# Delta-net opening: modulation groups pinned behind the products, small vectors turned sooner, first low parts of weights on VectorE

## Chip, cores and metric

One core of one Trainium2 chip runs the whole program. The metric is the device time of one execution in microseconds (us); lower is better. Engines: PE is TensorE, DVE is VectorE, ACT is ScalarE, POOL is GpSimd, SP is SyncE, which issues most of the transfers.

## What is computed

Two transformer blocks of two layers each, on 256 tokens of width 1024, all in float32. The part that matters here is the first layer of the first block:

```python
cond = jax.nn.silu(c)
mod = cond @ w_ada[layer] + b_ada[layer]                 # (1, 6144)
sh1, sc1, g1, sh2, sc2, g2 = jnp.split(mod[:, None, :], 6, axis=-1)
h = rms_norm(x, norm_mix[layer]) * (1.0 + sc1) + sh1
proj = h @ w_in                                          # gated delta net: (256,1024) @ (1024,4112)
qkv, z, a, b = jnp.split(proj, ...)
qkv = silu(causal_depthwise_conv(qkv, conv_w))           # 4 taps
...
```

The second block has its own modulation, `silu(c) @ w_ada[i] + b_ada[i]` and the same for `c_ctx`, from inputs that are there from the start, and ends each layer with a mixture of 16 experts.

## The kernel before

The program is written in Bass with the Tile framework. Its scheduler sets the order of the instructions of each engine from a simulated timeline. An instruction given to `keep_in_program_order` stays behind those of its engine that were written before it; instructions written under `issue_after(i)` come after instruction `i`.

**Exact products.** A product of float32 numbers is made of three products of parts: each weight is split by `split_w` (L380 to L392) into a high part `whi`, a cast on ACT (L387), and a low part `wlo`, a subtraction (L391) on VectorE, or on GpSimd where the counter `pool_next` is above zero (`gdn` sets it to 4 at L552) and for a share of all splits. The activations are split in the same way into `hi` and `lo`. The three matmuls of the delta net are L601 (hi by whi), L602 (hi by wlo) and L603 (lo by whi).

**The opening.** `rows_to_cols` and `runs_to_cols` (L168 to L194) load small vectors as rows and turn them into columns on PE (L178, L191) with a copy on VectorE (L180, L193): `va` and `vf` are the gains of the norms, `cw` the taps of the convolution; `al` comes of a matmul by ones in `gdn_consts` (L523). Meanwhile `ada_unit` makes the first third of the first layer's modulation: eight weight tiles of 128 x 2048 (1 MB each) are loaded by `load_w` (L135) into the raw buffers, and each goes through four matmuls of 32 rows (L218), called a group here. Then VectorE adds the bias (L244, `brow`), PE turns the result (L248), VectorE copies it (L250, `modc`) and forms the scale A (L364). `turned_early` has by then put the normed, turned x into PSUM; `modulated` makes `hi` on ACT (L371) and `lo` on VectorE in pairs (L372, L373).

**The delta net's projections** (`gdn`, L586 to L606) run over column blocks of 512 columns. A block has two raw tiles of 1 MB; each tile is split in two halves, and a half (two chunks of 128 rows by four of 128 columns) serves 24 matmuls, so that a block holds 96. After each block come the convolution of its columns (`conv`, ACT L559, VectorE L561), squares and, for later blocks, turns (L575, L580). Six such blocks are followed by `dense` for the rest.

**Background work.** `self.bg` is a list of generators; `fill` takes the next step of the first. While the delta net runs, the background is `ada2(0, 0)`, the second block's first modulation unit (`two` is true: eight groups of L218 that gather in one PSUM bank), and then further units on ACT and GpSimd.

**Buffers and queues.** All raw tiles come from one pool of five buffers in this stage (two, and `more_raw(3)`), shared by the delta net's weights and the modulation's. SP issues their loads one after another: a load whose buffer isn't free holds up the loads behind it. A delta-net tile's buffer comes free when its second low part is made, a modulation tile's when its group has run on PE.

Of the kernel before, what the change touches and what calls it, by code (L numbers as in the profile page):

```python
# [20 lines left out]
P = 128  # L21
# [11 lines left out]
class Kern:  # L33
# [134 lines left out]
    def rows_to_cols(self, name, srcs, eng=None):  # L168

        nc = self.nc  # L170
        n = sum(s.shape[0] for s in srcs)
# [5 lines left out]
        tp = self.tp()  # L177
        nc.tensor.transpose(tp[:, :n], r[:n, :P], self.ident[:n, :n])  # L178
        t = self.c.tile([P, n], F32, name=name)
        nc.vector.tensor_copy(t, tp[:, :n])  # L180
        return t

    def runs_to_cols(self, name, src, eng):

        nc = self.nc
        n = src.shape[0]
        r = self.t512()
        eng.dma_start(r[:n, :], src)
        tp = self.tp()
        for j in range(4):  # L190
            nc.tensor.transpose(tp[:, n * j:n * j + n], r[:n, j::4], self.ident[:n, :n])  # L191
        t = self.c.tile([P, 4 * n], F32, name=name)
        nc.vector.tensor_copy(t.rearrange("p (r j) -> p j r", j=4), tp[:, :4 * n].rearrange("p (j r) -> p j r", j=4))  # L193
        return t  # L194
# [11 lines left out]
    def ada_unit(self, w, b, unit, lhs, modc, two, dve=None, then=None, pool=False):  # L206
# [4 lines left out]
        if dve is None:  # L211
            bank = self.bank("ada")
            for k in range(KT):
# [3 lines left out]
                for j in range(4):  # L217
                    nc.tensor.matmul(bank[32 * j:32 * j + 32, :], lhs[:, k, :],  # L218
                                     r[:, 0, 512 * j:512 * j + 512], start=(k == 0), stop=(k == 7))
# [289 lines left out]
    def gdn_consts(self, bp):  # L509

        nc, I = self.nc, self.I
        am = self.t512()
        nc.gpsimd.dma_start(am[:, :2 * P], I["k_add"])
        mbf = bp.tile([P, 2 * P], BF16, name="mbf")
        nc.vector.tensor_copy(mbf, am[:, 0:2 * P])
        ibf = bp.tile([P, P], BF16, name="ibf")
        nc.vector.tensor_copy(ibf, self.ident)
# [4 lines left out]
        tp = self.tp()  # L522
        nc.tensor.matmul(tp[:, 0:16], self.ones[0:1, :], row, start=True, stop=True)  # L523
        nc.vector.tensor_copy(al[:, 0:16], tp[:, 0:16])
        cw = self.rows_to_cols("cw", [I["gdn_conv"][0].rearrange("a (r p) -> (a r) p", p=P), I["gdn_out_norm"]], nc.gpsimd)
        return mbf, ibf, al, cw

    def gdn(self, x, hi, lo, g1, consts, later):
# [3 lines left out]
        with ExitStack() as es:  # L532
# [19 lines left out]
            self.pool_next = 4  # L552
# [69 lines left out]
            self.banks("b", [2, 3], [], [7], [5])  # L622
            self.even_consts()
# [1368 lines left out]
    def prep(self):  # L1992
# [10 lines left out]
        self.va = self.rows_to_cols("va", [rv2(I[n]) for n in ("norm_mix", "norm_ffn", "norm_mix_2")], nc.gpsimd)  # L2003
        self.vf = self.runs_to_cols("vf", I["norm_ffn_2"].rearrange("l (h n) -> (l h) n", h=2), nc.gpsimd)
# [53 lines left out]
    def block1_layers(self, hp, modc, gb, ada, gmix, gffn):  # L2058
        I, x = self.I, self.x
        for l in range(2):  # L2060
            hi = hp.tile([P, KT, NTOK], F32R, name=f"hi{l}", tag="hi")
            lo = hp.tile([P, KT, NTOK], F32R, name=f"lo{l}", tag="lo")
            if l == 0:
                self.bg = [ada(0, 0, False)]
                consts = self.gdn_consts(self.accp)
                with self.more_raw(6), self.tc.tile_pool(reuse_waits="tile", name="xn", bufs=1, side="right") as xp:
                    early = self.turned_early(x, xp)
                    self.fill(5)
# [89 lines left out]
```

## Time and profile before

| | before |
|---|---|
| median of 3 runs | 2452.18 us (2449.21 to 2452.27) |
| profiled execution, its own time | 2443.09 us |
| span of the profiled execution | 2441.3 us |
| mean granted clock of PE | 0.941 |
| PE busy | 2123.6 us (87%) |
| VectorE busy | 1100.0 us (45%) |
| ScalarE busy | 773.9 us (32%) |
| GpSimd busy | 316.8 us (13%) |
| moved by DMA | 677.57 MB, mean 278 GB/s |

The time of an execution is a little above its span, which runs from the first to the last instruction. The profiled execution was 9 us below the median of the runs. A busy time is a union over an engine's instructions; the granted clock is a share of full speed (2.4 GHz), so 0.50 is 1.2 GHz. Line numbers in the profile are those of the kernel before; in the changed kernel the same lines have moved down by 3 to 13: L218 is L226 there, L244 is L254, L248 is L258, L372 and L373 are L382 and L383, L391 is L401, L387 is L397, L601 to L603 are L609 to L611.

### The profile page before, as it was taken

To read this page: it belongs to the slowest core of one execution; us is meant where nothing else is said; L and a number is where in the kernel's file an instruction comes from. 1 tells how busy PE (TensorE), PEld (TensorE's weight loads), DVE (VectorE), ACT (ScalarE), POOL (GpSimd) and SP (SyncE) were. 2 spreads that over 40 slices of the span, in tenths; PEclk is the share of its full clock that TensorE was granted. 3 is DMA by queue.
4 is the path that set the end of the run, shared out by engine and by line. 5 is a ranking of instruction groups with operands and counts; after the bars stand their busy time and mean duration, and the time that the engine had idled before them with its cause. 6 is when DMAs were issued, how large, how long until landed. Compare 5 with 4: busy or idle time off the path is not lost. (4 is left out here: it accounts for less than half of the span.)

```text
span 2441.3 us, 30277 instructions
## 1 busy us (share of the span) xinstructions
PE 2123.6 (87%) x12053; PEld 1278.1 (52%) x12053; DVE 1100.0 (45%) x2051; ACT 773.9 (32%) x1470; POOL 316.8 (13%) x334
## 2 busy tenths in 40 slices
PE   6987998998999979998988998888888987777777
PEld 3864676786677657885575222222265652222222
DVE  3777357866555575547764121212157731101111
ACT  3564344443555544435443100000047530000000
POOL 3344211112000040003411000000021010000000
PEclk8988998999999979999998999999989989989999
DMA  9657766976332356537746999999921469999998
GB/s 351 247 174 240 238 226 218 362 256 215 126 109 85 126 189 203 167 119 264 296 169 267 425 426 427 425 426 426 415 84 63 162 274 426 426 426 425 427 425 349
DMA packets 152445, 677.57 MB, mean 278 GB/s; under 512 B 15937, under 2 KB 38315, under 8 KB 113648
## 3 DMA queue, kind: packets, MB, share of 16 engines
q1 hardware_dynamic: 143072, 637.98, 67.3%
q0 software_dynamic: 6784, 36.48, 4.3%
q8 instruction: 95, 1.56, 0.3%
q10 hardware_dynamic: 2448, 1.18, 0.2%
q14 instruction: 46, 0.38, 0.0%
HBM read 667.07 MB, written 8.52 MB: 277 GB/s over the span
## 5 line engine op out<-in xcount | busy, mean ns | idle before, releaser
L391 DVE TENSOR_TENSOR wlo<-rawt,whi 128x1024 fp32r<-128x1024 f32 (+2 forms) x257 | 308.7, 1207 | 228.0 <-ACT whi L387 225.6
L387 ACT CAST whi<-rawt 128x1024 fp32r<-128x1024 f32 (+3 forms) x284 | 280.5, 995 | 313.7 <-PE mmt L398 118.9
L1872 PE MATMUL anyt<-rawb,xs 128*32 128x512 f32 x672 | 164.4, 650 | 52.0 <-DMA rawb<-in_w_exp_gate 26.7
L1858 PE MATMUL anyt<-rawb,xs 128*32 128x512 f32 x1472 | 175.2, 614 | 26.6 <-DMA rawb<-in_w_exp_up 17.3
L1832 DVE TENSOR_TENSOR y<-anyt,g 32x512 f32<-32x512 f32 (+1 forms) x120 | 66.4, 553 | 214.7 <-PE anyt L1825 206.9
L1825 PE MATMUL anyt<-rawb,hT 128*32 128x256 f32 (+1 forms) x1056 | 132.9, 491 | 21.2 <-DMA rawb<-in_w_exp_down 11.0
L398 PE MATMUL anyt<-whi,lo 128*128 128x512 f32 (+1 forms) x384 | 144.8, 379 | 1.8 <-DVE lo L333 1.8
L397 PE MATMUL anyt<-wlo,hi 128*128 128x512 f32 (+1 forms) x384 | 145.4, 380 | 1.1 <-DVE wlo L391 1.1
L1877 DVE TENSOR_TENSOR h<-anyt,h 64x512 f32<-64x512 f32 x16 | 11.1, 693 | 281.8 <-ACT h L1876 281.8
L396 PE MATMUL anyt<-whi,hi 128*128 128x512 f32 (+1 forms) x384 | 134.4, 381 | 0.4 <-ACT t L1723 0.4
L1876 ACT ACTIVATE h<-anyt 64x512 f32<-64x512 f32 x16 | 9.4, 589 | 392.4 <-PE anyt L1872 392.4
L1862 ACT ACTIVATE h<-anyt 128x512 f32<-128x512 f32 x16 | 9.6, 597 | 378.1 <-PE anyt L1858 378.1
L1872 PEld LDWEIGHTS anyt<-rawb,xs 128*32 128x32 f32 x672 | 39.3, 118 | 171.0 <-issue 100.7
L1858 PEld LDWEIGHTS anyt<-rawb,xs 128*32 128x32 f32 x1472 | 48.8, 112 | 147.1 <-issue 113.4
L1863 DVE TENSOR_TENSOR h<-anyt,h 128x512 f32<-128x512 f32 x16 | 11.1, 692 | 207.8 <-PE anyt L1858 207.8
L1825 PEld LDWEIGHTS anyt<-rawb,hT 128*32 128x32 f32 (+1 forms) x1056 | 49.5, 128 | 94.3 <-issue 65.0
L218 PE MATMUL adat<-rawt,lhs 128*32 128x512 f32 x448 | 73.6, 665 | 29.0 <-DMA rawt<-in_w_ada 24.9
L391 POOL TENSOR_TENSOR wlo<-rawt,whi 128x1024 fp32r<-128x1024 f32 (+1 forms) x27 | 67.6, 2511 | 237.7 <-ACT whi L387 196.2
L1872 PE MATMUL anyt<-rawt,xs 128*32 128x512 f32 x352 | 78.7, 596 | 10.9 <-DMA rawt<-in_w_exp_gate 7.3
L397 PEld LDWEIGHTS anyt<-wlo,hi 128*128 128x128 f32 x384 | 72.5, 189 | 20.5 <-issue 3.2
L398 PEld LDWEIGHTS anyt<-whi,lo 128*128 128x128 f32 x384 | 72.4, 188 | 16.2 <-DVE lo L333 2.2
L396 PEld LDWEIGHTS anyt<-whi,hi 128*128 128x128 f32 x384 | 71.6, 189 | 16.6 <-issue 0.8
(634 smaller groups left out, 4381.2 us busy)
## 6 DMA issues: line engine op xcount, KB each, us to landing
rawt<-in_w_ada SPq DMA_DIRECT2D x96, 1024.0 KB, 7.0
rawb<-in_w_exp_up SPq DMA_DIRECT2D x41, 2048.0 KB, 27.0
rawb<-in_w_exp_down SPq DMA_DIRECT2D x41, 2048.0 KB, 27.0
rawb<-in_w_exp_gate SPq DMA_DIRECT2D x39, 2048.0 KB, 25.6
rawt<-in_w_exp_gate SPq DMA_DIRECT2D x41, 1024.0 KB, 26.5
rawt<-in_w_ffn_in SPq DMA_DIRECT2D x40, 1024.0 KB, 7.7
rawt<-in_w_exp_up SPq DMA_DIRECT2D x38, 1024.0 KB, 27.0
rawt<-in_w_exp_down SPq DMA_DIRECT2D x31, 1024.0 KB, 27.0
```

The lines of the kernel that those rows point to most:

```text
L218: nc.tensor.matmul(bank[32 * j:32 * j + 32, :], lhs[:, k, :], r[:, 0, 512 * j:512 * j + 512], start=(k == 0), stop=(k == 7))
L387: nc.scalar.copy(hi, w)
L391: e.tensor_tensor(out=lo, in0=w, in1=hi.bitcast(F32), op=OP.subtract)
L396: nc.tensor.matmul(ps, xh, wh, start=start, stop=False)
L397: nc.tensor.matmul(ps, xh, wl, start=False, stop=False)
L398: nc.tensor.matmul(ps, xl, wh, start=False, stop=stop)
L1825: nc.tensor.matmul(yb[o:o + M, c:c + n], hT[:, k, :], w[:, i * n:i * n + n], start=(k == 0), stop=(k == KT - 1), **({} if S == 2 else dict ...
L1832: nc.vector.tensor_tensor(out=ys[s][p0:p0 + CAP, 256 * q:256 * (q + n)], in0=yb[o:o + CAP, c:c + 256 * n], in1=g2[o:o + CAP, 256 * q:256 * ...
L1858: nc.tensor.matmul(b[CAP * i:CAP * i + CAP, :], lhs(k0 + j, i % 2), r[:, j, 512 * hf:512 * hf + 512], start=(k0 + j == 0), stop=(k0 + j == ...
L1863: nc.vector.tensor_tensor(out=h, in0=banks[1], in1=h, op=OP.mult)
L1872: nc.tensor.matmul(b[o:o + 32, :], lhs(k0 + j), r[:, j, 512 * hf:512 * hf + 512], start=(k0 + j == 0), stop=(k0 + j == KT - 1), tile_posit ...
L1877: nc.vector.tensor_tensor(out=h[0:64, :], in0=b[64:P, :], in1=h[64:P, :], op=OP.mult)
```

## The change

1. `rows_to_cols(later=True)`, `runs_to_cols` and `gdn_consts` no longer turn their vectors where they load them; they give back a `turn` function. `block1_layers` calls these for `va`, `vf`, `al` and `cw` right after `turned_early`, with the PE instructions kept in program order, and lets most of the first modulation unit come after the last of them.
2. In `ada_unit`, where `two` is true, the four matmuls of the first group (k = 0) are kept in program order. Since the eight groups gather in one bank, the others follow the first.
3. `k_add`'s load and the casts `mbf` and `ibf` move from `gdn_consts` to the end of the projections.
4. `pool_next = 4` is gone: the first four low parts are made on VectorE.

```diff
--- before.py
+++ after.py
@@ -165,7 +165,7 @@
         self.tc.keep_in_program_order(self.nc.scalar.preload_act_table_set("natural_log_exp_and_others"))
 
 
-    def rows_to_cols(self, name, srcs, eng=None):
+    def rows_to_cols(self, name, srcs, eng=None, later=False):
 
         nc = self.nc
         n = sum(s.shape[0] for s in srcs)
@@ -174,24 +174,32 @@
         for s in srcs:
             (eng or nc.sync).dma_start(r[o:o + s.shape[0], :P], s)
             o += s.shape[0]
-        tp = self.tp()
-        nc.tensor.transpose(tp[:, :n], r[:n, :P], self.ident[:n, :n])
         t = self.c.tile([P, n], F32, name=name)
-        nc.vector.tensor_copy(t, tp[:, :n])
-        return t
+
+        def turn():
+            tp = self.tp()
+            i = nc.tensor.transpose(tp[:, :n], r[:n, :P], self.ident[:n, :n])
+            if later:
+                self.tc.keep_in_program_order(i)
+            nc.vector.tensor_copy(t, tp[:, :n])
+            return i if later else t
+        return (t, turn) if later else turn()
 
     def runs_to_cols(self, name, src, eng):
+
 
         nc = self.nc
         n = src.shape[0]
         r = self.t512()
         eng.dma_start(r[:n, :], src)
-        tp = self.tp()
-        for j in range(4):
-            nc.tensor.transpose(tp[:, n * j:n * j + n], r[:n, j::4], self.ident[:n, :n])
         t = self.c.tile([P, 4 * n], F32, name=name)
-        nc.vector.tensor_copy(t.rearrange("p (r j) -> p j r", j=4), tp[:, :4 * n].rearrange("p (j r) -> p j r", j=4))
-        return t
+
+        def turn():
+            tp = self.tp()
+            for j in range(4):
+                self.tc.keep_in_program_order(nc.tensor.transpose(tp[:, n * j:n * j + n], r[:n, j::4], self.ident[:n, :n]))
+            nc.vector.tensor_copy(t.rearrange("p (r j) -> p j r", j=4), tp[:, :4 * n].rearrange("p (j r) -> p j r", j=4))
+        return t, turn
 
 
     def ada_bias(self, b, c0, two):
@@ -215,8 +223,10 @@
                     yield
                 r = self.load_w(w[k * P:k * P + P, c0:c0 + 2048], 1, 2048)
                 for j in range(4):
-                    nc.tensor.matmul(bank[32 * j:32 * j + 32, :], lhs[:, k, :],
-                                     r[:, 0, 512 * j:512 * j + 512], start=(k == 0), stop=(k == 7))
+                    i = nc.tensor.matmul(bank[32 * j:32 * j + 32, :], lhs[:, k, :],
+                                         r[:, 0, 512 * j:512 * j + 512], start=(k == 0), stop=(k == 7))
+                    if two and k == 0:
+                        self.tc.keep_in_program_order(i)
         else:
             bank = self.bank("ada")
             for h in range(2):
@@ -509,20 +519,19 @@
     def gdn_consts(self, bp):
 
         nc, I = self.nc, self.I
-        am = self.t512()
-        nc.gpsimd.dma_start(am[:, :2 * P], I["k_add"])
         mbf = bp.tile([P, 2 * P], BF16, name="mbf")
-        nc.vector.tensor_copy(mbf, am[:, 0:2 * P])
         ibf = bp.tile([P, P], BF16, name="ibf")
-        nc.vector.tensor_copy(ibf, self.ident)
         al = bp.tile([P, 24], F32, name="al")
         row = bp.tile([1, 16], F32, name="alrow")
         nc.gpsimd.dma_start(row[:, 0:8], I["gdn_a_log"])
         nc.gpsimd.dma_start(row[:, 8:16], I["gdn_dt_bias"])
-        tp = self.tp()
-        nc.tensor.matmul(tp[:, 0:16], self.ones[0:1, :], row, start=True, stop=True)
-        nc.vector.tensor_copy(al[:, 0:16], tp[:, 0:16])
-        cw = self.rows_to_cols("cw", [I["gdn_conv"][0].rearrange("a (r p) -> (a r) p", p=P), I["gdn_out_norm"]], nc.gpsimd)
+
+        def turn():
+            tp = self.tp()
+            self.tc.keep_in_program_order(nc.tensor.matmul(tp[:, 0:16], self.ones[0:1, :], row, start=True, stop=True))
+            nc.vector.tensor_copy(al[:, 0:16], tp[:, 0:16])
+        cw, tw = self.rows_to_cols("cw", [I["gdn_conv"][0].rearrange("a (r p) -> (a r) p", p=P), I["gdn_out_norm"]], nc.gpsimd, True)
+        self.turns += [turn, tw]
         return mbf, ibf, al, cw
 
     def gdn(self, x, hi, lo, g1, consts, later):
@@ -549,7 +558,6 @@
             esd.enter_context(self.more_raw(3, "right", "gdn"))
 
             self.accv = dp
-            self.pool_next = 4
             a0 = self.bg[0]
             self.bg.insert(0, self.prep2_step(hi[:, 0, 0:1].bitcast(F32)))
 
@@ -620,6 +628,10 @@
             self.use_exp_ln()
             self.banks("a", [0, 1], [4], [6], [5])
             self.banks("b", [2, 3], [], [7], [5])
+            am = self.t512()
+            nc.gpsimd.dma_start(am[:, :2 * P], I["k_add"])
+            nc.vector.tensor_copy(mbf, am[:, 0:2 * P])
+            nc.vector.tensor_copy(ibf, self.ident)
             self.even_consts()
             cp = es.enter_context(tc.tile_pool(reuse_waits="tile", name="ctxp", bufs=1))
 
@@ -2000,8 +2012,9 @@
         x = self.c.tile([P, 2, D], F32, name="x")
         self.x = x
         nc.scalar.dma_start(x, I["x"][0].rearrange("(t p) d -> p t d", p=P))
-        self.va = self.rows_to_cols("va", [rv2(I[n]) for n in ("norm_mix", "norm_ffn", "norm_mix_2")], nc.gpsimd)
-        self.vf = self.runs_to_cols("vf", I["norm_ffn_2"].rearrange("l (h n) -> (l h) n", h=2), nc.gpsimd)
+        self.va, ta = self.rows_to_cols("va", [rv2(I[n]) for n in ("norm_mix", "norm_ffn", "norm_mix_2")], nc.gpsimd, True)
+        self.vf, tf = self.runs_to_cols("vf", I["norm_ffn_2"].rearrange("l (h n) -> (l h) n", h=2), nc.gpsimd)
+        self.turns = [ta, tf]
         lhs = self.c.tile([P, 8, 2, 16], F32, name="lhs2")
         nc.vector.tensor_copy(lhs, sc[:, 8:24].rearrange("p (s k) -> p k s", s=2).unsqueeze(3).to_broadcast([P, 8, 2, 16]))
         self.lhs2 = lhs.rearrange("p k s r -> p k (s r)")
@@ -2065,7 +2078,11 @@
                 consts = self.gdn_consts(self.accp)
                 with self.more_raw(6), self.tc.tile_pool(reuse_waits="tile", name="xn", bufs=1, side="right") as xp:
                     early = self.turned_early(x, xp)
-                    self.fill(5)
+                    for turn in self.turns:
+                        last = turn()
+                    self.fill()
+                    with self.tc.issue_after(last.ins):
+                        self.fill(4)
             m = modc[l][:, 0, :]
             if l:
                 self.norm_T(x, gmix(l), m[:, 8:16], m[:, 0:8], hi, lo, (0, 1))
```

What moves is seen in the order of the instructions on three engines (the scheduler sets it anew).

PE around the first products: `adat` with `lhs1` is the first layer's modulation, `adat` with `lhs2` the second block's, `tpt` a turn, `mmt` with `whi` or `wlo` a product. Before:

```order
L218 MATMUL adat_234<-rawt_271,lhs1_115 32x512 x4
L178 MATMUL tpt_95<-cst_68,t512_91 128x48
L523 MATMUL tpt_138<-alrow_135,cst_68 128x16
L218 MATMUL adat_234<-rawt_277,lhs1_115 32x512 x4
L191 MATMUL tpt_101<-cst_68,t512_99 128x4 x4
L248 MATMUL tpt_284<-cst_68,brow_231 128x128 x4
L178 MATMUL tpt_144<-cst_68,t512_141 128x97
L218 MATMUL adat_684<-rawt_685,lhs2_108 32x512 x4
L601 MATMUL mmt_355<-hi0_126,whi_359 128x256
```

After the change, the same place, and behind the line of dots what stands behind the 288th product:

```order
L181 MATMUL tpt_224<-cst_68,t512_125 128x97
L226 MATMUL adat_230<-rawt_243,lhs1_106 32x512 x4
...
L226 MATMUL adat_230<-rawt_273,lhs1_106 32x512 x4
L258 MATMUL tpt_280<-cst_68,brow_227 128x128 x4
L609 MATMUL mmt_351<-hi0_117,whi_355 128x256
...
L226 MATMUL adat_680<-rawt_681,lhs2_99 32x512 x4
L226 MATMUL adat_680<-rawt_687,lhs2_99 32x512 x4
L226 MATMUL adat_680<-rawt_693,lhs2_99 32x512 x4
L226 MATMUL adat_680<-rawt_699,lhs2_99 32x512 x4
L588 MATMUL tpt_833<-cst_68,kT_338 128x128 x2
```

The four turns stand ahead of the second modulation group; the first group of the second block's unit has gone from ahead of the first product to behind 288 products, and the other seven with it: four stand there together, one 24 products later, three within the 24 after that. Before, one stood ahead of the products, one within the first block, two behind 192 products and four behind 288.

SP's loads from the second block's third weight tile on (`in_w_ada_2` is the second block's modulation, `in_gdn_w_in` the delta net's weights; in brackets the DMA queues and engines whose count the issue waits for). Before:

```order
L135 DMA rawt_711<-in_gdn_w_in 128x4x512 [waits DMAHW6_49,DMAHW1_49,PE_49]
L135 DMA rawt_697<-in_w_ada_2 128x2048 [waits DMAHW7_49,Pool_49]
L135 DMA rawt_883<-in_w_ada_2 128x2048 [waits DMAHW2_49,DMAHW0_49,PE_49]
L135 DMA rawt_703<-in_w_ada_2 128x2048 [waits DVE_49]
L135 DMA rawt_769<-in_gdn_w_in 128x4x512 [waits DVE_49]
L135 DMA rawt_901<-in_w_ada_2 128x2048 [waits DMAHW6_49,DMAHW3_49,DVE_49]
L135 DMA rawt_889<-in_w_ada_2 128x2048 [waits DMAHW7_49,DMAHW4_49,PE_49]
L135 DMA rawt_895<-in_w_ada_2 128x2048 [waits DMAHW5_49,DMAHW1_49,PE_49]
L135 DMA rawt_917<-in_gdn_w_in 128x4x512 [waits DMAHW2_49,DVE_49]
L135 DMA rawt_1110<-in_gdn_w_in 128x4x512 [waits DMAHW6_49,DVE_49]
L135 DMA rawt_975<-in_gdn_w_in 128x4x512 [waits DMAHW0_49,PE_49]
```

After:

```order
L135 DMA rawt_693<-in_w_ada_2 128x2048 [waits DMAHW6_49,DVE_49]
L135 DMA rawt_699<-in_w_ada_2 128x2048 [waits DMAHW7_49,DVE_49]
L135 DMA rawt_707<-in_gdn_w_in 128x4x512 [waits DMAHW0_49,DVE_49]
L135 DMA rawt_765<-in_gdn_w_in 128x4x512 [waits DMAHW1_49,DMAHW0_49,DVE_49]
L135 DMA rawt_897<-in_w_ada_2 128x2048 [waits DMAHW2_49,DMAHW1_49,DVE_49]
L135 DMA rawt_913<-in_gdn_w_in 128x4x512 [waits DMAHW3_49,PE_49]
L135 DMA rawt_879<-in_w_ada_2 128x2048 [waits DMAHW4_49,PE_49]
L135 DMA rawt_885<-in_w_ada_2 128x2048 [waits DMAHW6_49,DMAHW5_49,PE_49]
L135 DMA rawt_891<-in_w_ada_2 128x2048 [waits DMAHW7_49,PE_49]
L135 DMA rawt_1106<-in_gdn_w_in 128x4x512 [waits DMAHW3_49,DVE_49]
L135 DMA rawt_971<-in_gdn_w_in 128x4x512 [waits DMAHW4_49,PE_49]
```

The third block's two tiles (711 and 769 before, 707 and 765 now) have moved behind two modulation loads. 707 now waits for the last low part of the second block (`wlo_609`), 765 for the last low part of 707 itself (`wlo_738`), so for the buffer that 707 had. The fourth block's first tile (917, now 913) waited for VectorE and now waits for the first pinned group (`rawt_681`); its second tile (975, now 971) waits for the fifth group, `rawt_879` (before, for its counterpart 883, which ran earlier).

VectorE at the opening (`brow` is the bias add, `wlo` a low part). Before:

```order
L180 COPY va_97<-tpt_95 128x48
L524 COPY al_134<-tpt_138 128x16
L193 COPY vf_106<-tpt_101 128x4x4
L515 CAST mbf_130<-t512_128 128x256
L244 TENSOR_TENSOR brow_231<-adat_234,brow_231 128x512
L250 COPY modc0_117<-tpt_284 128x4x4
L364 SCALAR_TENSOR_TENSOR smt_297<-modc0_117,va_97 128x8
L372 TENSOR_SCALAR t512_299<-hi0_126,modc0_117 128x256
```

After:

```order
L201 COPY vf_98<-tpt_215 128x4x4
L401 TENSOR_TENSOR wlo_356<-rawt_353,whi_355 128x1024
L532 COPY al_121<-tpt_221 128x16
L401 TENSOR_TENSOR wlo_384<-rawt_353,whi_383 128x1024
L401 TENSOR_TENSOR wlo_414<-rawt_411,whi_413 128x1024
L184 COPY cw_128<-tpt_224 128x97
L254 TENSOR_TENSOR brow_227<-adat_230,brow_227 128x512
L260 COPY modc0_108<-tpt_280 128x4x4
L374 SCALAR_TENSOR_TENSOR smt_293<-modc0_108,va_95 128x8
L382 TENSOR_SCALAR t512_295<-hi0_117,modc0_108 128x256
```

The first three low parts stand ahead of the bias add on VectorE. On ACT the cast for the third (`whi_413`) now stands behind the table load and the exponential of `al`, which before came ahead of all casts.

## Rows read from the trace of the kernel before

**Rows 1.** Windows: stretch, its us, busy PE, PEld, DVE, ACT, POOL (x), clock, DMA, GB/s

```profile
40.00:50.00 10.00, 9.36 (x61) 7.69 (x62) 3.40 (x10) 2.78 (x5) 5.49 (x10) 0.73 0.90 321
...
50.00:110.00 60.00, 59.90 (x500) 53.37 (x499) 41.58 (x73) 32.71 (x57) 18.40 (x19) 1.00 0.72 264
...
110.00:170.00 60.00, 46.35 (x280) 39.16 (x279) 51.63 (x93) 40.56 (x64) 29.34 (x14) 0.87 0.55 177
```

**Rows 2.** Timeline of the opening: start us, us, engine line op out<-in xcount [idle before <-releaser]

```profile
10.56 1.28 ACT L644 ACT_TABLE_LOAD   x1
...
28.46 0.21 ACT L644 ACTIVATE al<-al 128x8 f32<-128x8 f32 x1 [16.62 <-DVE al L524]
...
30.34 1.99 ACT L387 CAST whi<-rawt 128x1024 fp32r<-128x1024 f32 x2 [1.67 <-DMA rawt<-in_gdn_w_in]
...
30.97 0.68 DVE L244 TENSOR_TENSOR brow<-adat,brow 128x512 f32<-128x512 f32 x1
...
31.47 7.01 POOL L391 TENSOR_TENSOR wlo<-rawt,whi 128x1024 fp32r<-128x1024 f32 x3 [23.13 <-ACT whi L387]
...
33.09 0.76 DVE L364 SCALAR_TENSOR_TENSOR smt<-modc,va 128x8 f32<-128x8 f32 x1
...
34.58 1.70 DVE L372 TENSOR_SCALAR t<-hi,modc 128x256 f32<-128x256 f32 x1 [0.73 <-ACT hi L371]
...
36.76 2.58 DVE L372 TENSOR_SCALAR t<-hi,modc 128x256 f32<-128x256 f32 x2
...
39.66 0.34 DVE L372 TENSOR_SCALAR t<-hi,modc 128x256 f32<-128x256 f32 x1
...
40.32 0.34 DVE L372 TENSOR_SCALAR t<-hi,modc 128x256 f32<-128x256 f32 x1
...
40.65 1.94 PE L218 MATMUL adat<-rawt,lhs 128*32 128x512 f32 x8 [7.66 <-DMA rawt<-in_w_ada]
...
42.51 0.58 PE L601 MATMUL mmt<-hi,whi 128*128 128x256 f32 x1
```

**Rows 3.** Timelines of SP (issues) and ACT (casts of what landed)

```profile
42.64 0.37 SPq L135 DMA_DIRECT2D rawt<-in_gdn_w_in  x1
...
63.95 0.38 SPq L135 DMA_DIRECT2D rawt<-in_gdn_w_in  x1
...
78.37 10.09 SPq L135 DMA_DIRECT2D rawt<-in_gdn_w_in  x3
...
83.69 2.00 ACT L387 CAST whi<-rawt 128x1024 fp32r<-128x1024 f32 x2 [4.45 <-DMA rawt<-in_gdn_w_in]
```

**Rows 4.** Costliest groups: busy us, mean ns of one | idle before

```profile
L391 DVE TENSOR_TENSOR wlo<-rawt,whi 128x1024 fp32r<-128x1024 f32 (+2 forms) x257 | 308.7, 1207 | 228.0 <-ACT whi L387 225.6
```

**Rows 5.** Timeline of PE: modulation groups ahead of the third and fourth block

```profile
70.17 1.92 PE L218 MATMUL adat<-rawt,lhs 128*32 128x512 f32 x16
...
85.73 3.64 PE L218 MATMUL adat<-rawt,lhs 128*32 128x512 f32 x32
```

**Rows 6.** Windows of L601 alone, by column block: stretch, us, busy PE (x), clock

```profile
42.40:57.40 15.00, 9.74 (x34) 0.90 0.72 243
...
57.40:72.00 14.60, 8.70 (x31) 1.00 0.68 240
...
72.00:89.25 17.25, 9.22 (x32) 1.00 0.59 218
...
89.25:104.05 14.80, 8.99 (x32) 1.00 1.03 397
```

**Rows 7.** Loads of the delta net's weights, 20 to 100 us: time from issue to landing

```profile
DMA to landing us min/median/max: 5.2/7.6/20.6
```

**Rows 8.** Timeline of PE in the second block's first mixer

```profile
1103.93 3.36 PE L218 MATMUL adat<-rawt,lhs 128*32 128x512 f32 x16 [4.79 <-DMA rawt<-in_w_ada]
...
1110.93 1.07 PE L218 MATMUL adat<-rawt,lhs 128*32 128x512 f32 x8 [1.72 <-DMA rawt<-in_w_ada]
...
1114.25 1.94 PE L311 MATMUL tpt<-cst,xn 128*128 128x128 f32 x8 [2.26 <-DVE smt L159]
```

## Prediction, made before the change was run

> **What bounds the kernel now.** I read the table of windows first. From 50 to 110 us PE is busy 59.90 of 60 us at full clock, and from 110 to 170 it is busy 46.35 while VectorE has 51.63 [rows 1]: the delta net's projections are bound by PE, what follows by a mixture in which VectorE leads. So whatever stops PE before 110 is paid in full there, and 60 − 46.35 = 13.65 us of idle PE later could give some back. Then the timeline of the opening [rows 2]: PE waits 7.66 us for a transfer ahead of the group at 40.65, which belongs to the second block and not to the delta net; the first product starts when that group has run, at 42.51. This wait is what the pin is aimed at. But beside it VectorE is late too: its first L372 takes 1.70 us and the next two 2.58 us together while GpSimd makes three low parts (31.47 to 38.48), where one takes 0.34 us afterwards. Then SP's issues and the casts that wait for what they bring [rows 3]: they tell how early a weight must be issued.
>
> **The opening, step by step.** The order after the change puts three low parts ahead of the bias add on VectorE. The two casts for the first two end at 30.34 + 1.99 = 32.33; then come the table load, 1.28, and the exponential, 0.21 (before, at 10.56 and 28.46), and the third cast, 1.0: 34.8 [rows 2]. Its low part takes 1.2 on VectorE [rows 4], so 36.0, the copy of the taps some 0.25, and the bias add starts at about 36.3 where it started at 30.97: 5.3 us later. From the bias add to the first L372 it took 34.58 − 30.97 = 3.6; of that the scale A took 0.76 beside GpSimd, which I put at 0.15 without it: 3.0, so 39.3. Pairs of L372 and L373 then follow at 40.32 − 39.66 = 0.66. The first product's PSUM bank is free after five pairs and one more L372: 5 x 0.66 + 0.34 = 3.6. The first product: 43.0 for 42.51, **+0.5**. So the 7.66 us wait goes, and 5.3 us of low parts take its place; without GpSimd beside it VectorE is 4 us quicker behind the bias add. If the table load finds room elsewhere, it is 1.5 less (−1.0); if the pairs don't speed up, 3.2 more, being 1.70 + 2.58 − 3 x 0.34.
>
> **The clock of the first products.** The group at 40.65 took 1.94 us, two such groups 1.92 at full clock [rows 2, 5]: PE ran at 1.2 GHz after its wait, and the stretch 40 to 50 had a granted clock of 0.73 [rows 1]. Now the products come first; I let 1.94 us of them run at half speed in that group's place: **+0.9** (0 to 2).
>
> **The projections, block by block.** A block is 96 matmuls (32 of L601; the four stretches show 34, 31, 32 and 32 [rows 6]). The second took 14.60 us with two groups, 1.92 [rows 5]: 12.7, or 6.3 for the half that one raw tile serves. The third took 17.25 − 3.64 = 13.6 and the fourth 14.8 with more turns and sums in them; in the new order those fall into waits, so I go by 6.3 and keep (13.6 − 12.7) + (14.8 − 12.7) = 3.0 as an upper end. A raw tile takes 83.69 − 78.37 = 5.3 us from issue to the start of its cast [rows 3], then 1.0 and 1.2 to its first low part, another 1.1 to its second.
>
> The group of the first block (0.96) and the two of the second have gone from their places. The third block is thus ready at 72.0 + 0.5 + 0.9 − 2.9 = 70.5. Before, its first tile was loaded at 42.64, right after the first of the groups, and only its second waited for the last low part of the second block, at 63.95 [rows 3]. Now four of five buffers hold modulation weights by then, whose groups stand behind 288 products, so the *first* is the one issued at about 64.0: cast 69.3, low part 71.5, a stall of **1.0**. The second tile waits for the first one's own buffer, free at 72.6: cast 77.9, low part 80.1. PE is through with the first at 71.5 + 6.3 = 77.8, a stall of **2.3**. Block three ends at 86.4, and four groups run, to 90.0. The first of them, done at 87.3, is what releases the fourth block's first tile: cast 92.6, low part 94.8, a stall of **4.8** in which turns and sums fit. Twenty-four products and one group later, 94.8 + 3.1 + 1.0 = 98.9, its second tile is issued: low part 106.4, where PE, with 24 more products and three groups, is ready at 105.0: **1.4**. Block four then ends at 106.4 + 6.3 = 112.7 for 104.05: **+8.6**. With a tile of the median time to landing, 7.6 where the shortest is 5.2 [rows 7], the last step adds 2.4 more.
>
> Of this I let the stretch behind it give back **2.5**: VectorE's own backlog is shorter when the projections end late. The bounds are nothing and all 8.6, since PE idles 13.65 there.
>
> **The second block's mixers.** The pin holds for every unit with `two`. In the first mixer groups that ran for 3.36 and 1.07 us inside waits for weights (4.79 and 1.72 long) come behind the turns, which themselves wait for VectorE at 1114.25 [rows 8]. Those 4.4 us of PE work move into the products behind; other gaps take most of it: **+1.5**, between −6.5, if the turns were held by the two waits, and +4.4.
>
> The other edits I put at nothing. The turns of the small vectors are the same instructions in other places, on a PE that waits for weights between its modulation groups; what they can delay is a 1 us group with more than 1 us of waiting around it. `k_add` and the two casts aren't needed before the projections end. GpSimd loses four low parts and is not what PE waits for.
>
> **Sum.** 8.6 − 2.5 + 1.5 = +7.6 on the profiled execution's 2443.09. That one lies 9 us below the median, so I add the sum to the median: 2452.2 + 7.6, **2460 us**. About 0.2%, 4.9 us, is what a measurement of this kernel can tell from no change.
>
> **Rivals.**
> *Absorbed* (2453): the stall is 8.6 us but 110 to 170 us takes all of it; only the mixer's 1.5, or less, is left. For it: 13.65 us of idle PE. Against: VectorE is busy 51.63 of those 60 us, and its work there needs the products that come late.
> *Faster* (2447): in the first mixer of the second block the turns stand in PE's queue behind groups that wait 4.79 and 1.72 us for weights; pinned behind them, the groups no longer hold them up, 6.5 us at most. It decides if the stall at the projections is absorbed as above and at least 5 of the 6.5 us are real. Against: the turns last waited for VectorE, not PE [rows 8].
> *The clock falls again* (2465). In the trace a PE that had waited 7.66 us came back at 1.2 GHz, and 40 to 50 us had 0.73 of the clock: about 2.5 us lost. The two longest new waits, 4.8 and 2.3, would each cost that again: 7.6 + 5 = 12.6. Against: PE does turns and sums inside the longer one. [...]
> *The change doesn't do what it says*: the small vectors are turned earlier, but nothing waited for them; that part is nothing in every case above.
>
> **How the numbers follow.** Chances: forecast 0.55 (2454 to 2465 by the bounds: less or more given back, the slower tile, the mixer), absorbed 0.2, faster 0.1, clock 0.15. Leaving out the fast rival and the upper part of the clock's, the range is 2450 to 2468. Slower than 2457.1: most of the forecast, 0.52, and nearly all of the clock, 0.14, so 0.66. Faster than 2447.3: 0.12, the fast rival and a little of the absorbed. The rest, 0.22, is within.
>
> **What would show it.** Right: no wait of 7.66 us before the first product, which still starts near 43; bias add near 36; L382 at 0.34 from the start; PE waiting for `wlo` or `whi` in blocks three and four, at about 70, 78, 90 and 105 us, 9 to 10 us in all; the 385th product near 112.7. Wrong: the fourth block's first tile issued before 80 us; a first product before 41; PE busy throughout 50 to 110 as now; or the later stretches giving back or losing more than 5 us.

## The result, and the profile after

The change makes the kernel slower: 2465.85 us (median of 6 runs, 2457.85 to 2469.51) for 2450.28 before (median of 6), a ratio of 1.0063 with a 95% interval of 1.0043 to 1.0083, so 15.6 us more. The profiled execution took 2468.82 us, its span was 2467.0, the mean granted clock 0.936.

The windows of the changed kernel (stretch, its us, busy PE, PEld, DVE, ACT, POOL, clock, DMA share, GB/s) against [rows 1], with the four stretches in which the time is lost:

```profile
40.00:50.00 10.00, 7.53 (x42) 7.56 (x43) 4.49 (x14) 3.05 (x5) 4.21 (x8) 0.59 0.70 213
50.00:110.00 60.00, 54.41 (x400) 47.42 (x398) 30.66 (x54) 20.91 (x36) 9.03 (x13) 0.89 0.55 192
110.00:170.00 60.00, 48.66 (x335) 42.39 (x333) 48.99 (x93) 41.04 (x62) 28.54 (x16) 0.89 0.72 239
...
70.00:80.00 10.00, 6.72 (x53) 6.35 (x53) 6.94 (x13) 4.31 (x9) 0.61 (x1) 0.94 0.34 107
80.00:90.00 10.00, 10.00 (x66) 9.62 (x70) 3.83 (x7) 1.51 (x5) 2.65 (x3) 0.72 0.31 105
90.00:100.00 10.00, 7.79 (x56) 4.90 (x49) 7.14 (x14) 4.67 (x9) 2.53 (x4) 0.79 0.85 325
100.00:110.00 10.00, 10.00 (x62) 6.97 (x61) 0.42 (x1) 0.00 (x0) 0.23 (x1) 0.86 0.84 296
```

From 50 to 110 us PE did 400 matmuls where it had done 500. Two things are to be seen: it is idle for 5.6 us of the 60, and the clock, 1.00 before, is 0.89. Over the four stretches from 70 to 110 us the clock falls short by 0.06 + 0.28 + 0.21 + 0.14, which is 6.9 us of full speed; some 1.1 of it lies in PE's own waits and costs nothing, so that 5.8 are lost.

The opening, in the timeline, against [rows 2]:

```profile
29.75 1.99 ACT L397 CAST whi<-rawt 128x1024 fp32r<-128x1024 f32 x2 [19.60 <-DMA rawt<-in_gdn_w_in]
31.76 1.28 ACT L656 ACT_TABLE_LOAD   x1
34.23 1.23 DVE L401 TENSOR_TENSOR wlo<-rawt,whi 128x1024 fp32r<-128x1024 f32 x1 [0.96 <-ACT whi L397]
35.54 0.68 DVE L254 TENSOR_TENSOR brow<-adat,brow 128x512 f32<-128x512 f32 x1
38.52 0.41 DVE L382 TENSOR_SCALAR t<-hi,modc 128x256 f32<-128x256 f32 x1 [0.70 <-ACT hi L381]
42.47 0.55 PE L609 MATMUL mmt<-hi,whi 128*128 128x256 f32 x1 [5.08 <-DVE lo L383]
```

The 7.66 us wait for modulation weights is gone, and the first product starts when it did, 42.47 for 42.51: VectorE's bias add comes at 35.54 instead of 30.97, behind three low parts. L382 takes 0.41 us at once where L372 took 1.70 beside GpSimd. The Trainium skill, "SBUF — State Buffer", section "Who interferes with whom", says that an operation such as this `tensor_scalar` can take the ports that VectorE shares with GpSimd for its whole length, and that whichever of the two engines comes second then waits. The two rows agree, and so does the run below with the low parts back on GpSimd, where the first L382 takes 1.00 us and the next two 2.63 together.

PE's waits in column blocks three and four, then the casts that wait for weights there:

```profile
70.74 0.39 PE L610 MATMUL mmt<-hi,wlo 128*128 128x256 f32 x1 [0.75 <-DVE wlo L401]
78.69 0.69 PE L609 MATMUL mmt<-hi,whi 128*128 128x256 f32 x2 [1.97 <-ACT whi L397]
79.95 0.58 PE L610 MATMUL mmt<-hi,wlo 128*128 128x256 f32 x1 [0.57 <-DVE wlo L401]
89.34 3.64 PE L226 MATMUL adat<-rawt,lhs 128*32 128x512 f32 x32
97.03 0.80 PE L609 MATMUL mmt<-hi,whi 128*128 128x256 f32 x2 [1.75 <-ACT whi L397]
98.29 0.58 PE L610 MATMUL mmt<-hi,wlo 128*128 128x256 f32 x1 [0.46 <-DVE wlo L401]
...
112.79 0.66 PE L258 MATMUL tpt<-cst,brow 128*128 128x128 f32 x4 [0.82 <-DVE brow L254]
...
115.15 0.39 PE L610 MATMUL mmt<-hi,wlo 128*128 128x256 f32 x1 [1.47 <-DVE wlo L401]
```

```profile
62.94 9.29 SPq L135 DMA_DIRECT2D rawt<-in_gdn_w_in  x2
90.47 0.37 SPq L135 DMA_DIRECT2D rawt<-in_gdn_w_in  x1
...
77.59 1.99 ACT L397 CAST whi<-rawt 128x1024 fp32r<-128x1024 f32 x2 [3.10 <-DMA rawt<-in_gdn_w_in]
95.93 1.99 ACT L397 CAST whi<-rawt 128x1024 fp32r<-128x1024 f32 x2 [1.87 <-DMA rawt<-in_gdn_w_in]
```

The first tile of block four is issued at 90.47 where it was at 78.37 [rows 3]: right after the first of the four groups that start at 89.34. The products by block, L609 alone (stretch, us, busy PE (x), clock), against [rows 6]:

```profile
42.40:56.20 13.80, 10.25 (x32) 0.79 0.57 173
56.20:69.40 13.20, 9.06 (x33) 1.00 0.49 160
69.40:96.90 27.50, 9.74 (x32) 0.86 0.43 147
96.90:120.50 23.60, 9.69 (x33) 0.88 0.94 345
```

Blocks one and two are 2.6 us shorter together, without their three groups; three and four take 51.1 us for 32.05. Below, "the 385th product" is the first of the fifth block, counted in each trace: 104.09 us before, 120.63 now.

### The profile page after: what moved, and what is told of

The parts are those of the page before. It is cut to its first block, busy times and chain, and to the rows that moved or that the text cites. A ratio compares the mean times of both kernels' runs of the same rounds, so it can differ in the third digit from the quotient of the medians.

```text
span 2467.0 us, 30275 instructions
## 1 busy us (share of the span) xinstructions
PE 2123.3 (86%) x12053; PEld 1288.2 (52%) x12053; DVE 1097.5 (44%) x2055; ACT 773.5 (31%) x1470; POOL 305.5 (12%) x330
## 5 line engine op out<-in xcount | busy, mean ns | idle before, releaser
L401 DVE TENSOR_TENSOR wlo<-rawt,whi 128x1024 fp32r<-128x1024 f32 (+3 forms) x261 | 317.0, 1221 | 245.2 <-ACT whi L397 244.7
L1870 PE MATMUL anyt<-rawb,xs 128*32 128x512 f32 x1472 | 174.1, 611 | 32.7 <-DMA rawb<-in_w_exp_up 17.6
L1884 PE MATMUL anyt<-rawb,xs 128*32 128x512 f32 x672 | 158.3, 634 | 44.1 <-DMA rawb<-in_w_exp_up 22.2
L1837 PE MATMUL anyt<-rawb,hT 128*32 128x256 f32 (+1 forms) x1056 | 136.9, 505 | 25.7 <-DMA rawb<-in_w_exp_down 15.3
L401 POOL TENSOR_TENSOR wlo<-rawt,whi 128x1024 fp32r<-128x1024 f32 (+1 forms) x23 | 57.4, 2498 | 202.7 <-ACT whi L397 171.8
L408 PEld LDWEIGHTS anyt<-whi,lo 128*128 128x128 f32 x384 | 72.9, 190 | 16.5 <-DVE lo L343 2.2
L406 PEld LDWEIGHTS anyt<-whi,hi 128*128 128x128 f32 x384 | 72.0, 190 | 16.5 <-ACT t L1735 0.9
L407 PE MATMUL mmt<-wlo,hi 128*128 128x512 f32 (+1 forms) x192 | 77.7, 406 | 1.5 <-DVE wlo L401 1.5
```

The lines of the kernel that those rows point to most:

```text
L401: e.tensor_tensor(out=lo, in0=w, in1=hi.bitcast(F32), op=OP.subtract)
L406: nc.tensor.matmul(ps, xh, wh, start=start, stop=False)
L407: nc.tensor.matmul(ps, xh, wl, start=False, stop=False)
L408: nc.tensor.matmul(ps, xl, wh, start=False, stop=stop)
L1837: nc.tensor.matmul(yb[o:o + M, c:c + n], hT[:, k, :], w[:, i * n:i * n + n], start=(k == 0), stop=(k == KT - 1), **({} if S == 2 else dict ...
L1870: nc.tensor.matmul(b[CAP * i:CAP * i + CAP, :], lhs(k0 + j, i % 2), r[:, j, 512 * hf:512 * hf + 512], start=(k0 + j == 0), stop=(k0 + j == ...
```

## Experiments

All runs are set against the kernel before on the same chip; its median there was 2443 to 2447 us. "Unpinned" is the changed kernel without the pin. The ratio is given with its 95% interval.

**The pin taken away.** Of the change all is left but

```diff
-                    if two and k == 0:
-                        self.tc.keep_in_program_order(i)
```

> The changed kernel without the pin on the second block's first group. Theory A (the pinned groups hold four of five raw buffers, so the weights of column blocks three and four come late, and PE, idle for them, falls to 1.2 GHz): in the order two groups stand ahead of the first product and wait for their loads, so the first product starts near 45 us instead of 42.5, but the wait of PE for casts in blocks three and four is gone, the clock stays at 1.00 from 60 to 110 us, the 385th product comes at 104 to 108 us (120.6 with the change, 104.1 before), and the time is 2448 to 2456. Rival B (the low parts on VectorE and the turns are what costs): the time stays within 4 us of the changed kernel's 2466.

Measured: 2439.79 us, 0.9973 (0.9959 to 0.9986): faster than both. The 385th product comes at 102.69, the clock is 1.00 from 50 to 110 us, and PE has no wait between the groups ahead of the products and 110 us. Its windows and its waits at the opening:

```profile
50.00:110.00 60.00, 60.00 (x516) 55.67 (x515) 43.95 (x84) 34.72 (x58) 18.70 (x19) 1.00 0.73 266
```

```profile
40.11 1.93 PE L226 MATMUL adat<-rawt,lhs 128*32 128x512 f32 x8 [2.77 <-DMA rawt<-in_w_ada]
42.49 1.94 PE L226 MATMUL adat<-rawt,lhs 128*32 128x512 f32 x8 [0.44 <-DMA rawt<-in_w_ada]
```

The first product is late, 44.35 us, and it doesn't matter: two groups are over by then and their buffers free. Theory A was right in kind and not in size: the 385th product is 1.3 us sooner than it said, and the time 8 us below the range that I gave it. A second time:

> The changed kernel without the pin once more, beside the next two runs on one chip. If its 0.9973 was the kernel's and not that chip's, the ratio comes again at 0.996 to 0.999 and the 385th product at 102 to 104 us.

Measured: 2440.56, 0.9974 (0.9960 to 0.9987); the 385th product at 104.71, just outside what I expected.

**The pin alone**, put into the kernel before (the two lines above, with `i =` in front of the matmul).

> The kernel before with the pin alone; small vectors and low parts as before. Theory A: the order of loads is that of the changed kernel, so the 385th product comes at 118 to 122 us and the time is 2460 to 2468; the first product starts at about 41.7, when its PSUM bank is free. Rival B: the pin only takes away the 7.66 us wait, and the time is 2445 to 2452.

Measured: 2462.75, 1.0072 (1.0054 to 1.0089); first product 41.20, 385th 119.87, clock 0.91, 0.75 and 0.76 in the three stretches from 70 to 100 us. One line makes the whole loss; B falls.

**The low parts back on GpSimd.**

```diff
             self.accv = dp
+            self.pool_next = 4
             a0 = self.bg[0]
```

> The changed kernel with the first four low parts back on GpSimd. Theory A: the bias add comes back to about 31 us and the first product starts at 41.5 to 42.5, no more than 1 us sooner than with the change, since GpSimd slows VectorE's pairs again; the stalls of blocks three and four stay, and the time is 2463 to 2468. Rival B: the time falls by 5 us or more, to 2461 or less.

Measured: 2459.98, 1.0059 (1.0038 to 1.0079), the ratio of the changed kernel within its interval; first product 41.42, 385th 116.75. In microseconds that is B's number, 2461 or less; but the kernel before was itself 4 us faster on this chip, and the ratio doesn't tell this kernel from the changed one, so no gain is shown. The stalls stay, as A said. Of the 3.9 us by which the 385th product is sooner 2.2 are there at product 193 (67.31 for 69.48); the rest is the clock: block three has the same waits here (0.76, 1.92 and 0.76 us), but

```profile
70.00:80.00 10.00, 7.32 (x61) 7.03 (x61) 6.93 (x14) 4.13 (x8) 2.66 (x3) 1.00 0.41 118
80.00:90.00 10.00, 9.89 (x87) 6.96 (x85) 5.34 (x14) 3.21 (x8) 2.45 (x4) 1.00 0.54 188
90.00:100.00 10.00, 7.46 (x32) 5.78 (x32) 3.47 (x5) 2.41 (x3) 0.97 (x2) 0.66 1.01 401
```

the clock holds until the next long wait, 1.72 us ahead of block four. One more profile of each kernel was taken for this:

> The changed kernel once more, one profile. In its first profile PE's granted clock was 0.72 from 80 to 90 us and the 385th product came at 120.6; with the low parts back on GpSimd the same two waits (1.9 and 0.8 us) stood in block three, the clock stayed at 1.00 there, and the product came at 116.8. Theory L (whether the clock falls at that wait differs from execution to execution): another profile may show 1.00 from 80 to 90 and the 385th product at 116 to 118. Theory M (the order of the changed kernel decides it): 0.70 to 0.78 again and 120 to 121.

> The changed kernel with the low parts on GpSimd once more, one profile. Theory L: the clock may fall at the wait near 76 us this time, and the 385th product come at 119 to 121. Theory M: clock 1.00 from 70 to 90 again and the 385th product at 116 to 118.

Measured: the changed kernel had 0.83, 0.73 and 0.93 in the three stretches from 80 to 110, and the 385th product at 119.37; the other 1.00 and 0.66 from 80 to 100, and 116.58. The stretch from 80 to 90 in the changed kernel, then in the other:

```profile
80.00:90.00 10.00, 10.00 (x78) 8.71 (x80) 4.09 (x9) 2.34 (x6) 3.04 (x4) 0.83 0.31 105
...
80.00:90.00 10.00, 9.84 (x87) 6.91 (x85) 5.34 (x14) 3.20 (x8) 2.45 (x4) 1.00 0.56 193
```

As far as two profiles of each can tell, it goes with the kernel (M), not the execution. M's own numbers for the changed kernel, 0.70 to 0.78 and 120 to 121, were missed by a little.

**Two buffers held instead of four.** The pin stays.

```diff
-            for ci, rate in enumerate((1, 1, 2, 2, 2, 3)):
+            for ci, rate in enumerate((1, 1, 1, 2, 3, 3)):
```

> The changed kernel with the pin, where the background takes one step instead of two ahead of column block three (and three instead of two ahead of block five): two modulation tiles, not four, are written ahead of block three's weights, so two buffers are held behind the pin and not four. Theory A: both tiles of block three are loaded in time, the granted clock from 70 to 90 us is 0.95 or more, the 385th product comes at 104 to 112 us and the time is 2448 to 2457. Rival C (what costs is that PE runs all eight groups among the products of blocks four and five, with the loads as they are): the 385th product stays above 116 us and the time above 2461.

Measured: 2456.05, 1.0037 (1.0023 to 1.0051); no wait of PE over 0.4 us in block three or four, 385th product 108.57, and the clock holds:

```profile
50.00:110.00 60.00, 58.17 (x471) 49.29 (x469) 37.24 (x66) 28.94 (x47) 13.05 (x14) 1.00 0.68 239
```

So it is buffers, not the pin as such, that starve blocks three and four (C falls). A part of the remaining loss comes in block five: the 433rd product is at 121.80, where it was at 109.86. PE waits there 1.13 and 0.66 us for weights, 0.55 and 0.84 for the squares of its sums, and 2.01 ahead of the turns of the second block's bias add. By the 481st product 5.7 us of the lateness are left. The pin in the mixers is in this run too; the shares weren't separated.

**What the group is pinned behind.** `keep_in_program_order` ties an instruction to the last one of its engine that was *written* before it. That is no product: it is the last sum of squares of block two (L583), which waits for convolution, activation and square. In the order of the changed kernel PE has, ahead of the group:

```order
L583 MATMUL sct_330<-cst_68,sq_672 128x1 x2
L226 MATMUL adat_680<-rawt_681,lhs2_99 32x512 x4
```

and that sum stands behind product 288, though block two ends with product 192. The run queues the group behind product 48 and has no pin in the mixers:

```diff
-                    i = nc.tensor.matmul(bank[...], lhs[:, k, :], ...)
-                    if two and k == 0:
-                        self.tc.keep_in_program_order(i)
+                    with self.tc.issue_after(self.anchor) if two and k == 0 and self.anchor else ExitStack():
+                        nc.tensor.matmul(bank[...], lhs[:, k, :], ...)
```

> The first group of the delta net's unit is queued behind product 48 and not behind the last instruction that was written before it (a sum of squares, L583, which itself waits for convolution, activation and square of the second block). In the order four groups now stand behind product 192 and four behind 288. Theory A' (what costs is not that the group is queued behind products, but what it is queued behind): the buffers come free some 17 us sooner, no wait of PE for casts in blocks three and four beyond 1 us in all, clock 1.00 from 50 to 110, first product at 42.5, 385th product at 102 to 105, time 2437 to 2443. Rival E (any queueing behind the products starves the loads): the 385th product comes after 112 and the time is 2450 or more.

Measured: 2447.32, 1.0002 (0.9990 to 1.0013); 385th product 108.10. Better by some 12 us than the changed kernel at the 385th product, and yet neither theory's number: the scheduler puts four groups behind product 192, and PE still waits, 0.92 us in block four and 3.86 us at 130.97 in block six. Nor is the clock 1.00 from 50 to 110, as A' had it: it falls behind the short wait of block four.

```profile
93.44 0.39 PE L610 MATMUL mmt<-hi,wlo 128*128 128x256 f32 x1 [0.92 <-DVE wlo L401]
...
90.00:100.00 10.00, 9.02 (x63) 7.88 (x56) 8.00 (x13) 6.72 (x10) 2.17 (x2) 0.83 1.00 387
```

**The bias add ahead of the low parts**, on top of that: the first low part is queued behind the bias add, the next three behind the scale A.

```diff
-        e.tensor_tensor(out=lo, in0=w, in1=hi.bitcast(F32), op=OP.subtract)
+        with self.tc.issue_after(self.brow_add if self.nsplit == 1 else self.scale) if self.nsplit < 5 else ExitStack():
+            e.tensor_tensor(out=lo, in0=w, in1=hi.bitcast(F32), op=OP.subtract)
```

> As the run with the group behind product 48, and the first low part is queued behind the bias add, the next three behind the scale A. Theory F (with the group out of the way, three low parts ahead of the bias add are what sets the first product): the bias add starts at 30.3 to 31, the first product at 38.5 to 40, some 3 us sooner; the 385th product 2 to 3 us sooner than in that run, and the time 1 to 3 us less, 2435 to 2441. Rival G (the first product waits for something else, such as the casts on ACT, or the weights then come too late): first product later than 41, or the 385th product no sooner, and the same time within 1 us.

Measured: 2442.40, 0.9991 (0.9981 to 1.0001); first product 39.33, 385th 104.36. F holds for the products (3.1 and 3.7 us sooner than in the run above, the second a little more than F said); the ratio is lower by 0.0011, inside what the two intervals leave open.

**The pin in the mixers alone.** A counter leaves the first unit with `two` unpinned and pins all later ones.

```diff
-                    if two and k == 0:
+                    if two and k == 0 and self.first2 > 0:
```

> The changed kernel with the pin on every later unit of the second block's modulation but not on the first, so the delta net's loads and groups stand as in the run without a pin, and only the mixers of the second block differ from that run. Theory A (the pin costs in the delta net alone, some 20 us beside the unpinned kernel): 2438 to 2443, within 2 us of the unpinned run's ratio of 0.9973. Rival D (part of the loss is made in the mixers, where groups that ran in waits for weights move into the products, 1.5 to 4.4 us): 2442 to 2446, a ratio of 0.998 to 1.000.

Measured: 2445.92, 1.0003 (0.9992 to 1.0014), where the unpinned kernel has 0.9973 and 0.9974. D is right and was too small: 0.0030, some 7 us (3 to 12 by the two intervals). By the starts of matching ACT instructions in this profile and the two of the unpinned kernel, this kernel falls behind the first of these by 4.5 us across the first mixer, from 1100 to 1300 us, and by 2.6 between 1700 and 1900; behind the second by 2.7 and 5.5. PE runs no modulation group in that later stretch; what makes this part is open. In the second block's first mixer, against [rows 8], nothing of the background fills PE's waits any more:

```profile
1096.24 1.12 PE L300 MATMUL mmt<-t,cst 128*128 128x512 f32 x2 [1.48 <-POOL t L296]
1102.01 2.08 PE L300 MATMUL mmt<-t,cst 128*128 128x512 f32 x2 [4.65 <-POOL t L296]
1109.88 1.94 PE L323 MATMUL tpt<-cst,xn 128*128 128x128 f32 x8 [5.79 <-DVE smt L160]
```

**The turns alone**: unpinned, with `pool_next = 4` back.

> Without the pin, and with the first four low parts back on GpSimd: of the change only the sooner turns and the moved small loads are left. Theory H (without the pin the low parts on VectorE are what gains): the load of the second modulation tile waits for GpSimd's second low part and not VectorE's, so its group ends and the first product starts 1 to 3 us later than in the unpinned run (44.4), the 385th product at 104 to 106 us, and the ratio is 0.999 to 1.001. Rival I (the turns are what gains): the 385th product at 102 to 104 and the same ratio as the unpinned run.

Measured: 2440.07, 0.9978 (0.9967 to 0.9989): the ratio of the unpinned kernel, with the 385th product at 104.62, no sooner than in the kernel before. H falls: the low parts on VectorE don't gain the time. I's ratio is right and its reason not shown, as the products aren't sooner. What is left are the turns, the moved small loads and all that the scheduler then orders otherwise.

**Both.** Unpinned, bias first, and the first step of the second block's unit is taken after the first weight tile of block one, behind the turns of the bias add; the next two groups behind product 48, the third and fourth cast and low part behind `hi` and `lo`. The background takes one step instead of two ahead of block three. Of its edits, the one in the loop over the blocks:

```diff
+                    if (ci, k0) == (0, 4):
+                        for _ in range(1):
+                            next(a0)
                     if k0 % 4 == 0:
                         raw = self.load_w(W[k0 * P:k0 * P + 512, 512 * ci:512 * ci + 512], 4, 512)
```

> The way to have both: no pin in the mixers; the first two groups of the second block's unit are written, and their weights loaded, right after the delta net's first weight tile, queued behind the turns of the bias add (so they run while PE waits for hi), the next two behind product 48; the bias add ahead of the low parts, the third and fourth cast and low part behind hi and lo. Theory J (PE's wait at the opening is usable, if the groups' weights come before the delta net's later ones): loads of the two land near 33 and 36 us, the first product starts at 37.5 to 39.5, no wait for weights over 1 us in blocks one to four, the 385th product at 95 to 99 us, and, if half of that passes the stretch bound by VectorE, 2433 to 2439. Rival K (the later weight tiles are then late in blocks one and two, or what follows takes it all): the 385th product after 101 or the time within 2 us of the unpinned run's.

Measured: 2439.99, 0.9977 (0.9963 to 0.9990). The products do what J said:

```profile
28.96 0.66 PE L260 MATMUL tpt<-cst,brow 128*128 128x128 f32 x4 [0.87 <-DVE brow L255]
32.27 1.93 PE L229 MATMUL adat<-rawt,lhs 128*32 128x512 f32 x8 [2.66 <-DMA rawt<-in_w_ada]
34.66 1.94 PE L229 MATMUL adat<-rawt,lhs 128*32 128x512 f32 x8 [0.46 <-DMA rawt<-in_w_ada]
37.63 0.55 PE L621 MATMUL mmt<-hi,whi 128*128 128x256 f32 x1 [1.03 <-DVE lo L389]
```

Two groups run while PE waits for `hi`, the first product starts at 37.63, and the 385th is at 96.75, 7.3 us sooner than before and 8.0 than in the second unpinned run. The time is K's: 0.6 us from the unpinned run's. So an 8 us lead at 105 us is not there at the end. By the starts of matching ACT instructions it is 8 us at 100 to 130 us, 5.5 to 6 at 280, again 7.7 at 300 to 400, 3.6 at 1000 to 1100, and by the spans 1.4 at the end, one profile each. Why it shrinks wasn't tried.

## Why the prediction was right in direction, and where its sum failed

**Right.** The forecast named the mechanism: four buffers held behind the pin, the third block's first tile loaded at about 64 (62.94), its second waiting for the first one's buffer, the fourth's first released by the first group. Pin alone and pin away show it, and fewer held buffers move it. The opening came within 0.8 us at each step: bias add 35.54 for 36.3, first L382 38.52 for 39.3, first product 42.47 for 43.0. The waits in blocks three and four were to be 1.0, 2.3, 4.8 and 1.4 us, 9.5 in all, 9 to 10 by the list at the end. The first five in the fence above sum to 5.5, and 0.82 ahead of the bias turns at 112.79 and 1.47 at 115.15 make it 7.8: ahead of the fourth block 2.2 are left of 4.8, because the third ended some 3 us late and PE's turns and sums fill 92.9 to 95.3.

**Wrong: the clock's place.** I let the clock cost 0.9 us, at the first products, and left the rest to a rival with a chance of 0.15 and 5 us. At the first products it cost 1.4: it is at 0.50 until 48.1, where it was until 45.3. Between 70 and 110 us it fell short by 6.9 us of full speed, 5.8 of them while PE was busy, and by 5.1 in the second profile of the changed kernel (0.17 + 0.27 + 0.07). That is most of the distance from my 112.7 for the 385th product to 120.63 and 119.37. The rival's total, 2465, is where the median lies, though not for that reason alone.

The wait that the term and the rival took as their model, 7.66 us ahead of the group at 40.65, had not brought the clock down. In the kernel before it was as low ahead of that wait, with PE busy:

```profile
25.00:33.00 8.00, 6.52 (x28) 2.56 (x28) 1.49 (x6) 2.20 (x3) 1.53 (x1) 0.50 1.03 389
```

The Trainium skill ("TensorE: Matmul & The Clock Gate", section "Why this matters for your kernels") asks that PE be spared idle gaps between bursts of matmuls in mid-kernel, since they bring the lower clock. The gaps that it warns of are longer than any wait of PE between 50 and 110 us here, and the clock fell all the same; here the measurement decides.

**Wrong: "I let the stretch behind it give back 2.5".** Nothing came back. The 565th product was 18.1 us late (157.08 for 139.02), the 385th 16.5; in the second profile 16.6 and 15.3. Idle time of PE in a stretch that VectorE leads was no reserve. That the work of VectorE there hangs on the late products is my reading; no run tries it.

**Wrong in size: the mixers, +1.5.** The run with the pin there alone gives some 7 us. The sign was right; the size lies beyond my upper end of 4.4, though the interval takes it in. I had priced the first mixer alone, and its 2.7 to 4.5 us, by the ACT instructions, are near that upper end; what comes after 1700 us I had not counted.

**Wrong: "the other edits I put at nothing".** The unpinned kernel is 6.4 us faster than the kernel before (0.9974 of 2447). The turns and the moved loads, or the order that they bring about, gain that; where is open. In the profiles the products of the first five blocks don't show it.

**Wrong: turns and sums that vanish in waits.** From the first product to the 385th PE's own work, with the clock taken out, rose by 1.6 us (one group more, 0.96, is in it). In my sum it falls by 2.2, as I went by 6.3 us for every half block and kept 3.0 for the turns and sums as an upper end only.

**The sum, put right.** The 385th product is 16.5 us late for 8.6: 7.8 by waits, some 7.2 by the clock, 1.6 by work. Nothing comes back for 2.5, the mixers cost some 7 for 1.5, and the other edits gain 6.4 for nothing. If the parts simply add, that makes 17.1, for 15.6 measured with an interval of 10.5 to 20.3. The range held by luck: errors of both signs were in it.

The *absorbed* and the *faster* rival fall with the same runs: the stall is still there at 1100 us, where matching ACT instructions of the changed kernel's two profiles are 15.7 and 22.4 us late, and pinning in the mixer costs where the rival had it gain.

## What to carry to other kernels

An instruction queued behind others to keep it out of the way also holds its input's buffer for as long, and with a shared pool the loads behind it are the price: count the buffers held before the order of the engine. Look up what a pin ties to; here it was a late sum of squares and not a product, and a wait taken out of the front of a stretch bound by PE came back as several inside it, each of which can also cost the clock. Where a wait for background work is to go, bring its load forward into a gap that is already there, and see if the gain reaches the end before keeping it.

## What the hardware showed unexpectedly

Waits of nearly the same length were followed by different clocks. In block three, waits of 1.97 and 1.81 us in the changed kernel's two profiles, and of 1.92 and 1.77 in the two with the low parts on GpSimd, each had one of 0.57 to 0.76 us before and after it. From 80 to 90 us the clock was then 0.72 and 0.83 in the first kernel and 1.00 both times in the second. In the run with the group behind product 48 a single wait of 0.92 us was followed by 0.83 from 90 to 100 us; in the next run, with the bias add first, one of 0.93 left it at 1.00. The length of a wait alone doesn't tell whether the clock falls; what else does, these runs leave open.

A wait at the front of the products cost nothing by the fifth block: the unpinned kernel starts them at 44.4 to 45.5 us, 2 to 3 us later than the kernel before, and reaches the 385th within 1.4 us of it on either side.
